# A four-layer hybrid decoder trunk: block-wise norms in the first layer, another order of the PSUM reads of x, two weight loads moved, and a new plan of the last S5 layer

## The chip, the cores and the metric

The kernel runs on one core of a Trainium2 chip. TensorE (PE) multiplies, VectorE (DVE), ScalarE (ACT) and GpSimd (POOL) do the element-wise work, and SyncE (SP) does nothing but issue DMAs, one after the other in its own order. The metric is the device time of one execution in microseconds; less is better.

## The reference

Four layers, 512 positions, width 1024, fp32. Layer 0 and layer 3 are S5, layer 1 is HGRN2, layer 2 is sliding-window attention. Each layer does:

```python
u = rms_norm(h, norm_pre[i])
y = branch(u)                      # projection, causal mixer, gate, output projection
h = h + rms_norm(y, norm_post[i])

def rms_norm(x, g):
    return x * rsqrt(mean(x * x, axis=-1) + NORM_EPS) * g

# the S5 branch
proj = h @ w_in                    # 1024 x 2048
u, z = proj[..., :1024], proj[..., 1024:]
# 64 groups of 16 channels with 64 complex states: s[t] = a * s[t-1] + B u[t]; y = Re(C s) + D u
y = gelu(y)
y = y * sigmoid(y @ w_glu + b_glu)
out = (y * silu(z)) @ w_out
```

## The kernel before, in words

**Tiles.** Positions are cut into four blocks `tb` of 128. Every layer starts with the pre-norm of its input h (in layer 0 that is x itself). `norm_stats` squares each block on ACT with a running sum (`xs`, `pre_ss`), two short POOL instructions make 1/rms from the sum (`rs_m`, `rs_r`), and DVE scales the block into `xs`. `norm_xt` transposes `xs` on PE, 128x128 at a time, into a PSUM tile `xtp` that holds four transposed pieces; there are two such tiles in turn. ACT copies each piece out of PSUM as `xh` (the leading bits, with the norm's gain), and DVE writes the rest, `xl = xtp * gain - xh`. In layer 0 there is no `xl`: ACT writes plain fp32 `xf`. Matmuls with the weights `whi`/`wlo` (split in the same way, `w_conv`: ACT writes `whi`, DVE writes `wlo`) take three passes, `xh*whi`, `xl*whi`, `xh*wlo`.

**Weights.** `w_load` issues on SP the two DMAs of one weight chunk into `wraw`, whose buffers are reused, so a load can stand in SP's queue and wait until PE has read the old contents. `w_next` hands out the next chunk, and starts the load of later ones. Layer 0's `s5_in` chunks are used as they are (`plain`); all others are split.

**S5.** The projection gives u in eight blocks b of 128 channels. For each block: SP sends u through DRAM (`ub<-ut`, `u<-ub`); DVE makes `q` (713, 715) from the parameters `prm` (a DMA) and from it and the powers `ap` the tile `vt` (727 to 731); PE multiplies `kps<-vt,c`; PE transposes (`tps`, `ktp`); DVE masks `ksb`; eight DMAs on SP spread `ksb` into the block-Toeplitz matrix `toep`; PE makes the block inputs `xps<-u,v`, DVE rotates them, runs the scan `r` (line 835) and makes `spre` (845); PE adds up `yps<-toep,u` and `yps<-w,spre` (858, 860); ACT takes it out as `ysb` (gelu), PE transposes it back (`ytp`), ACT writes `y`, `yh`. Then comes the GLU projection `pj<-yh,...`.

**Order.** Engines run their instructions strictly in the order given. In the S5 layers that order comes from a hand-made planner (`Flow`): each piece of work is a list of steps with an engine, an estimated length and the marks it needs, and has a rank; the planner always emits the step that could begin first by its estimates, the rank breaking ties. Elsewhere the order follows the tile framework's scheduler. `out_proj` of one layer is interleaved with `norm_stats` and `norm_xt` of the next, in halves (blocks 0 and 1, then 2, then 3); `first_blocks` starts the next layer's projection on the first half.

Lines that matter: 274 squares, 277 scales `xs`, 253/254 the POOL steps, 292 `xtp`, 296 `xh`/`xf`, 298 `xl`, 228 `pj`, 152 weight loads, 182/183 `whi`/`wlo`, 706 `prm`, 691/692 and 613 `rotf`, 802/806 `ub`/`u`, 773 `toep`, 718 `c` (on ACT, from `prm`), 950 `yl`.

Of the kernel before, what the change touches and what calls it, by code (L numbers as in the profile page):

```python
# [15 lines left out]
ALU = mybir.AluOpType  # L16
# [4 lines left out]
KB = 8  # L21
# [29 lines left out]
class Mark:  # L51


    def __init__(self):
        self.t = None


class Flow:
# [6 lines left out]

    LAG = {"P": 0.4, "V": 0.4, "A": 0.4, "G": 0.4, "D": 4.5}

    def __init__(self):
        self.free = dict.fromkeys(self.LAG, 0.0)
        self.lines = []  # L70

    def add(self, line, rank, t=0.0):
# [36 lines left out]
class Trunk:  # L109
# [86 lines left out]
    def w_next(self, name=None):  # L196
        i = self.wi
        if name is not None:
            assert self.wseq[i][0] == name, (self.wseq[i], name)
        self.wi += 1  # L200
        self.w_conv(i)
        self.w_load(i + 1)
        if self.wseq[i][0].endswith("out") and self.wseq[i][2] == 1:
            return self.wcv.pop(i)
        if not self.plain(i) or self.plain(i + 1):
            self.w_conv(i + 1)
            self.w_load(i + 2)
        return self.wcv.pop(i)

    def w_take(self):  # L210
# [47 lines left out]
    def norm_stats(self, L, tbs, h):  # L258

        nc = self.nc  # L260
        if tbs[0] == 0:
            if L == 0:
                self.x = (self.act.tile([P, KB, T], F32, tag="xh", name="xf"), None)
            else:
                self.x = (
                    self.act.tile([P, KB, T], F32R, tag="xh", name="xh"),
                    self.act.tile([P, KB, T], F32R, tag="xl", name="xl"),
                )
            self.xs = self.act.tile([P, 4, D], F32, tag="z", name="xs")
        xs = self.xs  # L270
        n = len(tbs)
        ss = self.small.tile([P, 2], F32, tag="pre_ss", name="pre_ss", bufs=2)
        for i, tb in enumerate(tbs):
            self.last_sq = nc.scalar.activation(out=xs[:, tb, :], in_=h[:, tb, :], func=AF.Square, accum_out=ss[:, i:i + 1])
        r = self.rstd(ss[:, 0:n], D, n)
        for i, tb in enumerate(tbs):
            self.last_xs = nc.vector.tensor_scalar(out=xs[:, tb, :], in0=h[:, tb, :], scalar1=r[:, i:i + 1], scalar2=None, op0=ALU.mult)

    def norm_xt(self, L, tbs):

# [6 lines left out]
        for k2 in range(KB // per):  # L287
# [5 lines left out]
            for kk in range(per):  # L293
                k = per * k2 + kk
                g = self.gpre[:, L * KB + k:L * KB + k + 1]
                nc.scalar.activation(out=xh[:, k, c], in_=ps[:, kk, :], func=AF.Copy, scale=g)
                if xl is not None:
                    nc.vector.scalar_tensor_tensor(out=xl[:, k, c], in0=ps[:, kk, :], scalar=g, in1=xh[:, k, c].bitcast(F32), op0=ALU.mult, op1=ALU.subtract)  # L298
            yield

# [27 lines left out]
    def out_proj(self, L, nxt, h):  # L328
# [31 lines left out]
        with self.wx_pool(L):  # L360
# [14 lines left out]
                    spill(0)  # L375
            self.w_conv(self.wi)
            self.w_load(self.wi + 1)
            xt = iter(()) if nxt is None else self.norm_xt(nxt, (0, 1))
            next(xt, None)
            for tb in (2, 3):  # L380
# [238 lines left out]

    def s5_convs(self, i0, m):  # L620

        for c in range(1, 8):
            yield "A", 2.1, (m["cd", c - 2],) if c > 1 else ()
            yield "V", 2.6, ()
            self.w_conv(i0 + c)
            self.w_load(i0 + c + 1)
            yield m["cv", c]
# [360 lines left out]
    def layer_s5(self, L):  # L988
# [6 lines left out]
        with self.scratch("left"), self.tc.manual_schedule(engines={E.PE, E.DVE, E.Activation, E.SP}):  # L995
# [2 lines left out]
            m = defaultdict(Mark)  # L998
            ps, yh, yl, glu = {}, [], [], []

            flow = Flow()
            i0 = self.wi
            if j == 0:
                flow.add(self.s5_tables(j, m), 0, 5.0)
            else:
                m["ap"].t = 4.5
                flow.add(self.s5_convs(i0, m), 60)
            for b in range(8):
                flow.add(self.s5_core(b, m), 10 * b + 1)
# [478 lines left out]
    def run(self):  # L1488
        tc, nc, a = self.tc, self.nc, self.a
        self.plan_weights()  # L1490
        with tc.tile_pool(name="cst", bufs=1) as self.small, \
# [16 lines left out]
            for tb in range(4):  # L1508
                nc.sync.dma_start(out=x0[:, tb, :], in_=a["x"][tb * 128:(tb + 1) * 128, :])
                if tb == 1:  # L1510
                    self.w_load(0)
            for tbs in ((0, 1), (2,), (3,)):
                self.norm_stats(self.layers[0], tbs, x0)
            for _ in self.norm_xt(self.layers[0], (0, 1)):
                pass
            self.hsrc = a["x"].rearrange("(b p) d -> p b d", p=P)
# [125 lines left out]
```

## Time and profile before

| | us |
|---|---|
| median of three runs | 1119.49 (1118.13 to 1121.62) |
| the profiled execution, its own time | 1116.3 |
| its span in the trace | 1114.5 |
| PE busy in the span | 1031.2 (93%) |
| DVE busy | 750.5 (67%) |
| ACT busy | 504.2 (45%) |
| mean granted TensorE clock | 0.973 of full speed |

The time before the span starts and after it ends is 1.8 us. Rows of the timeline read: start, length, engine, line, operation, output<-inputs, and, in brackets, how long the engine had been idle before and what ended that.

### The profile page before, as it was taken

The numbers are of one execution on the slowest core, as the hardware profiler recorded it, in microseconds if no ns is written. First come the engines' busy times: TensorE is split into PE (matmuls) and PEld (weight loads), VectorE is DVE, ScalarE is ACT, GpSimd is POOL, SyncE is SP. The second block draws the span as 40 slices with busy tenths as digits, with TensorE's granted clock in tenths as the row PEclk, the third lists the DMA queues.
The fourth block names the chain that finished last, engine by engine and source line by source line (L and its number), as shares of the span: only waits on it lengthen the run. The fifth ranks groups of instructions, "written<-read, shape, count | busy, mean of one in ns | idle before, by whom it ended". The sixth has DMA issues, their size and how long they took to land.

```text
span 1114.5 us, 17031 instructions
## 1 busy us (share of the span) xinstructions
PE 1031.2 (93%) x6480; PEld 822.3 (74%) x6480; DVE 750.5 (67%) x1458; ACT 504.2 (45%) x933; POOL 103.2 (9%) x162
## 2 busy tenths in 40 slices
PE   5999975999999999999999898999997879988997
PEld 4755544778899798998978885666676767766876
DVE  6786759585698777887856565556664468863752
ACT  4344425554452314333244534688743355645540
POOL 2000000030200000000011022100002010100200
PEclk9999988999999999999999999999999889998999
DMA  6574233533432324414153452211125357544331
GB/s 230 137 190 126 74 85 98 171 114 126 143 103 81 114 71 132 144 65 151 61 189 124 122 145 62 74 57 53 61 95 167 117 155 238 173 124 146 104 103 57
DMA packets 70577, 133.31 MB, mean 120 GB/s; under 512 B 28896, under 2 KB 40032, under 8 KB 69472
## 3 DMA queue, kind: packets, MB, share of 16 engines
q1 hardware_dynamic: 65664, 119.04, 34.6%
q10 hardware_dynamic: 4832, 13.19, 3.6%
q8 instruction: 51, 0.84, 0.3%
q14 instruction: 30, 0.25, 0.1%
HBM read 100.51 MB, written 20.15 MB: 108 GB/s over the span
## 4 chain that ended last, share of the span: by engine, by line
PE 63%; DVE 15%; ACT 6%; DMA 6%; issue 5%; SPq 2%; POOL 1%; ACTq 1%; DVEq 0%; POOLq 0%
PE pj L228 26%; PE ops L243 13%; PE zps L243 4%; PE vps L243 3%; PE sps L1120 2%; PE scps L1328 2%; DVE wlo L183 2%; SPq L773 2%; ACT whi L182 2%; PE aops L1364 2%; DMA rsw<-rraw 1%; DMA prm<-in_s_bc 1%; PE ptp L1359 1%; DVE sg L1049 1%; PE yps L858 1%
## 5 line engine op out<-in xcount | busy, mean ns | idle before, releaser
L183 DVE TENSOR_TENSOR wlo<-wraw,whi 128x1024 fp32r<-128x1024 f32 x116 | 143.2, 1251 | 65.0 <-ACT whi L182 56.1
L228 PE MATMUL pj<-xh,whi 128*128 128x512 f32 (+1 forms) x496 | 182.3, 370 | 0.0
L228 PE MATMUL pj<-xl,whi 128*128 128x512 f32 (+1 forms) x496 | 177.9, 360 | 2.5 <-DVE xl L298 2.4
L228 PE MATMUL pj<-xh,wlo 128*128 128x512 f32 (+1 forms) x496 | 177.4, 359 | 0.0
L182 ACT ACTIVATE whi<-wraw 128x1024 fp32r<-128x1024 f32 x116 | 120.7, 1056 | 79.4 <-PE pj L228 38.2
L228 PE MATMUL pj<-xf,wraw 128*128 128x512 f32 (+1 forms) x320 | 116.0, 512 | 0.0
L228 PEld LDWEIGHTS pj<-xh,whi 128*128 128x128 f32 x496 | 96.3, 195 | 16.8 <-issue 5.8
L228 PEld LDWEIGHTS pj<-xl,whi 128*128 128x128 f32 x496 | 96.9, 196 | 14.6 <-DVE xl L298 3.2
L228 PEld LDWEIGHTS pj<-xh,wlo 128*128 128x128 f32 x496 | 96.5, 195 | 13.6 <-issue 1.7
L243 PE MATMUL ops<-whi,gh 128*128 128x512 f32 x256 | 101.6, 398 | 2.7 <-ACT gh L1051 2.2
L243 PE MATMUL ops<-wlo,gh 128*128 128x512 f32 x256 | 100.7, 394 | 1.1 <-DVE wlo L183 1.0
L243 PE MATMUL ops<-whi,gl 128*128 128x512 f32 x256 | 100.5, 395 | 0.0
L228 PEld LDWEIGHTS pj<-xf,wraw 128*128 128x128 f32 x320 | 59.2, 192 | 40.4 <-issue 36.7
L243 PEld LDWEIGHTS ops<-whi,gh 128*128 128x128 f32 x256 | 48.2, 188 | 13.8 <-ACT gh L1051 3.0
L243 PEld LDWEIGHTS ops<-wlo,gh 128*128 128x128 f32 x256 | 48.2, 188 | 13.2 <-DVE wlo L183 2.7
L243 PEld LDWEIGHTS ops<-whi,gl 128*128 128x128 f32 x256 | 48.1, 188 | 11.3 <-DVE gl L1052 0.9
L228 PE MATMUL pj<-yl,whi 128*128 128x512 f32 x128 | 51.0, 399 | 3.5 <-DVE yl L950 3.5
L228 PE MATMUL pj<-yh,whi 128*128 128x512 f32 x128 | 51.3, 401 | 0.5 <-ACT yh L946 0.5
L228 PE MATMUL pj<-yh,wlo 128*128 128x512 f32 x128 | 50.8, 397 | 0.0
L341 DVE TENSOR_TENSOR yg<-ops,gpost 128x512 f32<-128x512 f32 x32 | 21.9, 688 | 36.9 <-ACT junk L339 36.6
L243 PE MATMUL vps<-wlo,xh 128*128 128x256 f32 x160 | 45.3, 283 | 0.0
L243 PE MATMUL vps<-whi,xl 128*128 128x256 f32 x160 | 45.3, 283 | 0.0
(279 smaller groups left out, 2106.4 us busy)
## 6 DMA issues: line engine op xcount, KB each, us to landing
wraw<-in_s_in SPq DMA_DIRECT2D x32, 512.0 KB, 6.3
wraw<-in_hg_in SPq DMA_DIRECT2D x32, 512.0 KB, 3.6
wraw<-in_at_in SPq DMA_DIRECT2D x20, 512.0 KB, 4.2
wraw<-in_s_glu SPq DMA_DIRECT2D x16, 512.0 KB, 3.8
wraw<-in_s_out SPq DMA_DIRECT2D x16, 512.0 KB, 3.5
hd<-h SPq DMA_DIRECT2D x6, 1024.0 KB, 4.0
prm<-in_s_bc SPq DMA_DIRECT2D x16, 256.0 KB, 4.6
ub<-ut SPq DMA_DIRECT2D x16, 256.0 KB, 4.2
```

Source lines behind the costliest of these rows:

```text
L182: nc.scalar.activation(out=hi, in_=raw, func=AF.Copy)
L183: nc.vector.tensor_tensor(out=lo, in0=raw, in1=hi.bitcast(F32), op=ALU.subtract)
L228: self.nc.tensor.matmul(ps, lhsT=l[k // 4][:, k % 4, c], rhs=r[:, k, n0:n1], start=k == 0 and n == 0, stop=k == KB - 1 and n == len(terms) ...
L243: self.nc.tensor.matmul(ps, lhsT=l[:, k, c], rhs=r[k // per][:, k % per, :], start=k == 0 and n == 0, stop=k == KB - 1 and n == 2)
L341: nc.vector.tensor_tensor(out=yg[:, tb, f], in0=ps, in1=gp[:, f], op=ALU.mult)
L773: nc.sync.dma_start(out=toep[128 - n:128, jj, :, :], in_=ksb[0:n].rearrange("p a g h -> p (a g) h"))
L858: nc.tensor.matmul(o, lhsT=u[:, g, :], rhs=d["toep"][:, :, g, :], start=True, stop=False)
L1049: nc.vector.tensor_tensor(out=sg, in0=sg, in1=y[:, k, :], op=ALU.mult)
L1120: nc.tensor.matmul(ps[:, c, :], lhsT=k[:, c * 128:c * 128 + 128], rhs=q4[:, c, :, 1, :], start=True, stop=True)
L1328: nc.tensor.matmul(ps[:, bb, lo:256], lhsT=self.q[r, 4 * p + 2 * b2 + bb, qs], rhs=self.k[r, p, ks], start=True, stop=True)
L1359: nc.tensor.transpose(tp[:, f, bb, :], sm[:, bb, f * 128:f * 128 + 128], self.ident)
L1364: nc.tensor.matmul(ops[64 * i:64 * i + 64].rearrange("p b q -> p (b q)"), lhsT=self.v[:, n - 1 + f, kv * 64:kv * 64 + 64], rhs=pts[i][:, f ...
```

## The change

1. `norm_xt`: for each PSUM tile, first all ACT copies (`xh`), then all DVE differences (`xl`); before, the two were written in turns, piece by piece.
2. Layer 0 only: `norm_stats` runs for one block at a time (four calls instead of blocks 0 and 1 together, then 2, then 3), and the scaling into `xs` is an ACT instruction instead of a DVE one. The second weight chunk is also loaded before the second half of x.
3. `w_next`: a plain chunk starts the split and load of later chunks only if those are plain too. In layer 0 the first GLU chunk is thus loaded one step later.
4. `out_proj` before layer 3 also splits the next weight chunk and loads the one behind it.
5. The planner of layer 3: ACT counts as busy until 12.0 and DVE until 13.0, the powers `ap` as ready at 12.0 instead of 4.5, and the weight splits of `s5_convs` start at chunk 2 instead of 1.

```diff
@@ class Flow
-    def __init__(self):
+    def __init__(self, **busy):
         self.free = dict.fromkeys(self.LAG, 0.0)
+        self.free.update(busy)
@@ def w_next
-        if not self.plain(i) or self.plain(i + 1):
+        if not self.plain(i):
             self.w_conv(i + 1)
             self.w_load(i + 2)
+        elif self.plain(i + 1):
+            self.w_conv(i + 1)
+            if self.plain(i + 2):
+                self.w_load(i + 2)
@@ def norm_stats
-            self.last_xs = nc.vector.tensor_scalar(out=xs[:, tb, :], in0=h[:, tb, :], scalar1=r[:, i:i + 1], scalar2=None, op0=ALU.mult)
+            if L == 0:
+                nc.scalar.activation(out=xs[:, tb, :], in_=h[:, tb, :], func=AF.Copy, scale=r[:, i:i + 1])
+            else:
+                self.last_xs = nc.vector.tensor_scalar(out=xs[:, tb, :], in0=h[:, tb, :], scalar1=r[:, i:i + 1], scalar2=None, op0=ALU.mult)
@@ def norm_xt
                 nc.scalar.activation(out=xh[:, k, c], in_=ps[:, kk, :], func=AF.Copy, scale=g)
-                if xl is not None:
+            if xl is not None:
+                for kk in range(per):
+                    k = per * k2 + kk
+                    g = self.gpre[:, L * KB + k:L * KB + k + 1]
                     nc.vector.scalar_tensor_tensor(out=xl[:, k, c], ...)
@@ def out_proj
             self.w_load(self.wi + 1)
+            if nxt == 3:
+                self.w_conv(self.wi + 1)
+                self.w_load(self.wi + 2)
@@ def s5_convs
-        for c in range(1, 8):
+        m["cv", 1].t = 0.0
+        for c in range(2, 8):
@@ planner of the S5 layers
-            flow = Flow()
+            flow = Flow() if j == 0 else Flow(A=12.0, V=13.0)
-                m["ap"].t = 4.5
+                m["ap"].t = 12.0
@@ start of the program
                 if tb == 1:
                     self.w_load(0)
-            for tbs in ((0, 1), (2,), (3,)):
-                self.norm_stats(self.layers[0], tbs, x0)
+                    self.w_load(1)
+            for tb in range(4):
+                self.norm_stats(self.layers[0], (tb,), x0)
```

How this moves instructions is seen at three places. In the changed kernel's rows the line numbers are its own: 279 squares, 284 scales x, 305 is `xh`/`xf`, 311 is `xl`, 735 is `c`, 815 `ut`, 832 `mdec`, 819/823 `ub`/`u`, 723 `prm`, 153 the weight loads, 790 `toep`, 183 `whi`.

ACT at the start of the program, before, from the cosine table of layer 0 to the last `xf` of the first half; `x_98` is x:

```order
L421 ACTIVATE cos<-red_n,cst 128x96
L274 ACTIVATE xs,pre_ss<-x_98 128x1024 x2
L296 ACTIVATE xf<-xtp,gpre 128x256 x4
L1031 DMA bglu<-in_s_bglu 128x8
L296 ACTIVATE xf<-xtp,gpre 128x256 x4
```

and in the changed kernel:

```order
L437 ACTIVATE cos<-red_n,cst 128x96
L284 ACTIVATE xs<-x_98,rs_r 128x1024 x2
L305 ACTIVATE xf<-xtp,gpre 128x256 x2
L279 ACTIVATE xs,pre_ss<-x_98 128x1024
L305 ACTIVATE xf<-xtp,gpre 128x256
L284 ACTIVATE xs<-x_98,rs_r 128x1024
L279 ACTIVATE xs,pre_ss<-x_98 128x1024
L305 ACTIVATE xf<-xtp,gpre 128x256
L284 ACTIVATE xs<-x_98,rs_r 128x1024
L305 ACTIVATE xf<-xtp,gpre 128x256 x4
```

Two squares and all four scalings now stand between and ahead of the eight `xf` on the one engine.

SP in layer 0, before, from the `rotf` that follows block 3's `toep` to the `prm` after block 4's:

```order
L691 DMA rotf<-rot 64x1024
L692 DMA rotf<-rot 64x1024
L152 DMA wraw<-in_s_glu 128x1024 x2
L806 DMA u<-ub 128x512
L773 DMA toep<-ksb 16x128
...
L773 DMA toep<-ksb 128x128
L706 DMA prm<-in_s_bc 128x512
```

and in the changed kernel:

```order
L708 DMA rotf<-rot 64x1024
L709 DMA rotf<-rot 64x1024
L823 DMA u<-ub 128x512
L790 DMA toep<-ksb 16x128
...
L790 DMA toep<-ksb 128x128
L723 DMA prm<-in_s_bc 128x512
L153 DMA wraw<-in_s_glu 128x1024 x2
```

The GLU load has moved behind u, the eight `toep` DMAs and `prm`.

ACT at the start of layer 3, before, from the square of the last block on (`mdec` and `c` are S5 parameters, `junk` ends out_proj's norm):

```order
L339 ACTIVATE junk,po_ss<-ops 128x512
L274 ACTIVATE xs,pre_ss<-h 128x1024
L1031 DMA bglu<-in_s_bglu 128x8
L815 ACTIVATE mdec<-m_7713 128x8x63
L718 ACTIVATE c_7724<-prm,cst 128x8x16
L296 ACTIVATE xh<-xtp,gpre 128x128 x16
L748 ACTIVATE kt<-kps 128x256
L756 ACTIVATE v<-tps 128x512
L798 ACTIVATE ut<-pj 128x512
```

and in the changed kernel:

```order
L352 ACTIVATE junk,po_ss<-ops 128x512
L279 ACTIVATE xs,pre_ss<-h 128x1024
L1049 DMA bglu<-in_s_bglu 128x8
L305 ACTIVATE xh<-xtp,gpre 128x128 x16
L832 ACTIVATE mdec<-m_7730 128x8x63
L815 ACTIVATE ut<-pj 128x512
L735 ACTIVATE c_7741<-prm,cst 128x8x16
L183 ACTIVATE whi<-wraw 128x1024 x2
L815 ACTIVATE ut<-pj 128x512
```

The sixteen `xh` of blocks 2 and 3 now stand ahead of `mdec` and `c`. On DVE the same has happened, before:

```order
L277 TENSOR_SCALAR xs<-h,rs_r 128x1024
L713 TENSOR_TENSOR q_7805<-prm,co 128x256
L715 TENSOR_TENSOR q_7805<-q_7805,q12b 128x256
L727 TENSOR_TENSOR vt<-ap,q_7805 128x1024
L298 SCALAR_TENSOR_TENSOR xl<-xtp,gpre,xh 128x128 x8
L730 TENSOR_TENSOR t_7874<-ap,q_7805 128x1024
L731 TENSOR_TENSOR vt<-vt,t_7874 128x1024
L298 SCALAR_TENSOR_TENSOR xl<-xtp,gpre,xh 128x128 x8
```

and in the changed kernel:

```order
L286 TENSOR_SCALAR xs<-h,rs_r 128x1024
L311 SCALAR_TENSOR_TENSOR xl<-xtp,gpre,xh 128x128 x16
L730 TENSOR_TENSOR q_7931<-prm,co 128x256
L732 TENSOR_TENSOR q_7931<-q_7931,q12b 128x256
L744 TENSOR_TENSOR vt<-ap,q_7931 128x1024
L747 TENSOR_TENSOR t_7978<-ap,q_7931 128x1024
L748 TENSOR_TENSOR vt<-vt,t_7978 128x1024
```

The first `q`, `vt` and `t` of layer 3 come behind all sixteen `xl`.

## Rows read from the trace of the kernel before

**Rows 1.** The windows of the trace, busy time of each engine in five stretches (PE, PEld, DVE, ACT, POOL, each with its count of instructions), then the granted clock, the DMA share and GB/s: first the start, then layer 0 up to its block 4, then the end of layer 2's projection, the head of layer 3, and the rest of layer 3's mixer.

```profile
0.00:12.00 12.00, 0.06 (x1) 0.07 (x1) 4.28 (x18) 7.01 (x13) 4.41 (x22) 1.00 0.84 310
...
30.00:141.00 111.00, 110.26 (x688) 64.04 (x688) 82.49 (x106) 43.61 (x78) 5.80 (x10) 1.00 0.50 132
...
840.00:860.00 20.00, 16.19 (x119) 14.85 (x117) 10.05 (x14) 5.25 (x12) 5.78 (x16) 1.00 0.57 158
860.00:874.00 14.00, 8.83 (x47) 7.35 (x48) 9.04 (x20) 5.08 (x15) 0.62 (x1) 0.52 0.34 125
874.00:1016.00 142.00, 124.62 (x1101) 100.48 (x1100) 91.96 (x116) 80.67 (x127) 12.76 (x15) 0.97 0.60 179
```

**Rows 2.** The waits of PE, from 0 to 300 us: who waited for whom, us in total, times, longest.

```profile
PE xtp L292 <- DVE xs L277: 11.9, 1, 11.9
PE yps L858 <- DMA toep<-ksb: 9.1, 2, 7.6
```

**Rows 3.** The waits of PE, from 840 to 1045 us.

```profile
PE xtp L292 <- DVE xl L298: 6.4, 2, 4.9
PE kps L745 <- DVE vt L731: 5.3, 1, 5.3
PE pj L228 <- DVE yl L950: 3.5, 1, 3.5
```

**Rows 4.** The timeline of ACT at the start of the program (the square of block 2, then the first `xf`), of POOL (the mask, then the 1/rms of block 2), of DVE (block 2's scaling), and of PE (first transposes, the first half's matmuls, the next transposes).

```profile
11.03 1.06 ACT L274 ACTIVATE xs<-x 128x1024 f32<-128x1024 f32 x1 [1.23 <-DMA x<-in_x]
...
13.54 0.84 ACT L296 ACTIVATE xf<-xtp,gpre 128x256 f32<-128x256 f32 x2
...
9.50 0.40 POOL L766 TENSOR_TENSOR dmx<-dm,cst 128x128 f32<-128x128 f32 x1 [5.94 <-DMA cst<-in_const]
...
12.26 0.33 POOL L253 TENSOR_SCALAR rs_m<-pre_ss 128x1 f32<-128x1 f32 x1 [1.23 <-ACT xs L274]
...
13.25 0.75 DVE L277 TENSOR_SCALAR xs<-x,rs_r 128x1024 f32<-128x1024 f32 x1 [0.71 <-POOL rs_r L254]
...
11.94 2.21 PE L292 MATMUL xtp<-cst,xs 128*128 128x128 f32 x8 [11.94 <-DVE xs L277]
...
16.79 10.38 PE L228 MATMUL pj<-xf,wraw 128*128 128x256 f32 x46
27.00 1.04 PE L292 MATMUL xtp<-cst,xs 128*128 128x128 f32 x8
```

**Rows 5.** Layer 0, block 4: the timeline of SP, of DVE (the masked `ksb`; the last part of the scan's output `spre`), and of PE (a group of `yps` of block 3; the first of block 4).

```profile
122.83 19.52 SPq L152 DMA_DIRECT2D wraw<-in_s_glu  x2
...
142.91 5.00 SPq L773 DMA_DIRECT2D toep<-ksb  x8
...
131.84 0.29 DVE L768 TENSOR_TENSOR ksb<-ktp,dmx 128x128 f32<-128x128 f32 x1 [6.01 <-PE ktp L762]
...
141.37 0.68 DVE L845 TENSOR_TENSOR spre<-r,rsw 128x504 f32<-128x504 f32 x1
...
122.62 0.39 PE L858 MATMUL yps<-toep,u 128*64 128x128 f32 x4
...
149.59 0.69 PE L858 MATMUL yps<-toep,u 128*64 128x128 f32 x4 [7.62 <-DMA toep<-ksb]
```

**Rows 6.** The windows behind that, columns as in rows 1.

```profile
144.00:150.00 6.00, 0.41 (x4) 0.44 (x6) 5.16 (x8) 0.00 (x0) 0.00 (x0) 0.76 0.58 173
150.00:156.00 6.00, 6.00 (x41) 4.63 (x38) 0.00 (x0) 1.19 (x2) 0.00 (x0) 0.68 0.42 118
```

**Rows 7.** The timeline of PE where layers 1 and 2 begin (transposes of block 3), and the windows behind these.

```profile
306.54 0.66 PE L292 MATMUL xtp<-cst,xs 128*128 128x128 f32 x4 [2.59 <-DVE xl L298]
...
623.41 0.77 PE L292 MATMUL xtp<-cst,xs 128*128 128x128 f32 x5 [3.37 <-DVE xl L298]
...
306.00:312.00 6.00, 5.46 (x32) 5.18 (x33) 5.30 (x25) 4.94 (x13) 0.00 (x0) 0.72 0.00 1
...
624.00:630.00 6.00, 5.98 (x38) 5.74 (x37) 2.80 (x8) 2.88 (x8) 0.00 (x0) 0.72 0.00 1
```

**Rows 8.** The head of layer 3: the timeline of ACT (`c`, then the `xh` of block 2), of DVE (`xl`), of PE.

```profile
856.43 0.40 ACT L718 ACTIVATE c<-prm,cst 128x128 f32<-128x128 f32 x1 [4.58 <-DMA prm<-in_s_bc]
856.74 0.35 ACT L296 ACTIVATE xh<-xtp,gpre 128x128 fp32r<-128x128 f32 x1
859.45 0.37 ACT L296 ACTIVATE xh<-xtp,gpre 128x128 fp32r<-128x128 f32 x1 [2.36 <-DVE xl L298]
...
861.02 0.62 ACT L296 ACTIVATE xh<-xtp,gpre 128x128 fp32r<-128x128 f32 x2 [0.42 <-DVE xl L298]
...
859.85 0.35 DVE L298 SCALAR_TENSOR_TENSOR xl<-xtp,gpre,xh 128x128 fp32r<-128x128 f32 x1 [0.43 <-ACT xh L296]
...
861.83 1.11 PE L292 MATMUL xtp<-cst,xs 128*128 128x128 f32 x4 [4.87 <-DVE xl L298]
...
867.54 0.58 PE L228 MATMUL pj<-xl,whi 128*128 128x256 f32 x1 [1.76 <-DVE xl L298]
```

**Rows 9.** The timeline of DVE and of PE in layer 3, blocks 1 and 2, and of PE where the GLU's matmuls begin.

```profile
894.61 0.42 DVE L713 TENSOR_TENSOR q<-prm,co 128x256 f32<-128x256 f32 x1 [10.79 <-DMA prm<-in_s_bc]
...
905.49 1.08 PE L745 MATMUL kps<-vt,c 128*32 128x128 f32 x16 [5.32 <-DVE vt L731]
...
1015.48 0.80 PE L228 MATMUL pj<-yl,whi 128*128 128x512 f32 x1 [3.45 <-DVE yl L950]
```

## The prediction

> **What bounds the kernel now.** I first read the windows, for where PE stands still [rows 1]. From 30 to 141 us PE is busy 110.26 of 111 us, so whatever delays the start delays everything up to there. Layer 3 is the opposite: PE is idle 20.00 - 16.19 = 3.8 us at the end of the norm before it, 14.00 - 8.83 = 5.2 us in its head and 142.00 - 124.62 = 17.4 us in the rest of its mixer, 26.4 us together, and the head runs at a granted clock of 0.52, close to the lower of the two levels (1.2 of 2.4 GHz). Then I read PE's waits. Up to 300 us there are the first 11.9 us for x and, among others, 7.6 us in one wait for `toep` [rows 2]. In layer 3 they are transposes behind `xl`, `kps` behind `vt`, the GLU behind `yl` [rows 3]. The timelines then tell what stood in front of each awaited thing. Elsewhere the change touches PE only through the order of PSUM reads where layers 1 and 2 begin [rows 7].
>
> **The start of layer 0: a loss.** The first transposes began at 11.94, the 23 matmuls of blocks 0 to 2 ran without a gap from 16.79, and the next transposes stood at 27.00: (27.00 - 16.79) / 23 = 0.444 us each [rows 4]. In the changed order ACT does, after the cosine: two scalings, two `xf`, a square, an `xf`, a scaling, a square, an `xf`, a scaling, four `xf`. Splitting the sums of blocks 0 and 1 gives nothing, since POOL's 1/rms stands behind its mask, which waited for the constants until 9.50. A scaling on ACT I take at the 1.06 us of the square with the same shape; an `xf` is 0.84 / 2 = 0.42. From the end of a square to the scaling that uses it take 13.25 - (11.03 + 1.06) = 1.16 us, which is ACT's accumulator, POOL's two steps and the hand-over [rows 4]. With that: scalings to 12.7 (11.0 at the earliest, two of 1.06, overlapping a little), transposes, `xf` 0 and 1 from 13.5 to 14.4; square of block 2 to 15.5; `xf` 2 to 15.9; scaling of block 2 from 16.65 to 17.7; square of block 3 to 18.8; `xf` 3 to 19.2; scaling from 20.0 to 21.0; `xf` 4 from there, done at 21.45. PE's last four first-half transposes need the PSUM tile that `xf` 3 empties, so PE idles from about 16 to 19.2, does three matmuls of block 0 and waits again for `xf` 4. From 21.45 there are still 4 + 16 = 20 matmuls: 21.45 + 20 x 0.444 = 30.3 against 27.0, **+3.3 us**. The second weight chunk ahead of x's second half costs its 1 MB at 310 GB/s [rows 1], 3.4 us on block 2 of x (before, ACT took it at 11.03 on arrival): 14.4, just where ACT now wants it, so nothing more. DVE is freed of four scalings, but PE waits for none of DVE's work here: no gain.
> Such a pause lowers the clock: behind a PE gap of 2.59 us at 306.54 the next six microseconds showed a granted clock of 0.72, behind 3.37 us at 623.41 again 0.72 [rows 7], which is 6 x 0.28 = 1.7 us lost each time. Here two gaps of 3 and 1 us follow on a short activity. I add 1.3, between 0 (the one gap at 11.94 cost little) and 1.7 twice. Start: **+4.6**, from +2.5 (scalings as short as DVE's 0.75) to +6.7. The Trainium skill (TensorE: Matmul & The Clock Gate, Part 1: The HAM clock gate) speaks against this part: the throttled clock is the default and activity has to release it. By it a PE that stops in its first ten microseconds pays a low clock again; the rows at 306.54 and 623.41 agree, and the term would be nearer +5.
>
> **The GLU load moved behind `toep` in layer 0: a gain.** Block 4's `ksb` was ready at 131.84 + 0.29 = 132.1, but SP issued its `toep` only at 142.91, because the GLU load in front took 19.52 us from 122.83: its second half waited for a `wraw` buffer that PE was still reading. PE then stood still for 7.62 us until 149.59 [rows 5]. Behind it the clock was 0.76 and 0.68 in two six-microsecond windows, the first with PE idle [rows 6]; a group of `yps` took 0.69 instead of 0.39 [rows 5]. On 6.00 busy us at 0.68 that is 6.00 x 0.32 = 1.9 us. In the changed order u, the eight `toep` and `prm` precede the load. `toep` can go out at 132.2, its issue takes 5.00 [rows 5], and it lands by about 139, ahead of PE's arrival at 141.97. PE's next need, `spre`, is ready at 141.37 + 0.68 = 142.05: no new wait. The load itself then blocks the next block's u, which before went out after it as well. Gain **-9.3** (rounded down from 7.6 + 1.9), lower end 0 if something else on SP or DVE is late next, upper end -9.5. The Trainium skill (DMA: Bandwidth & Descriptors, Anatomy of one DMA) says that DMA engines don't wait on semaphores, the issuing sequencer does, before dispatch. The 19.52 us row agrees: one waiting load holds up all behind it.
>
> **PSUM reads, layers 1 and 2.** In turns, an `xh` comes every 860.2 - 859.45 = 0.78 us (ACT's idle 0.42 <-`xl` between two of 0.37), DVE idles 0.43 for each `xh`; two ACT copies without that wait take 0.62 for both, 0.31 each [rows 8]. Four pieces of a PSUM tile in turns are some 3.1 us; all `xh`, then all `xl`, some 1.2 + 0.2 + 1.2 = 2.6, and ACT goes on to the other tile meanwhile, so two tiles take about 1.2 + 2 x 1.2 + 0.4 = 4.0 instead of 6.2. Against it the first `xl` comes later by three copies, 0.9 us. Where layer 1 begins the wait was 2.59, in layer 2 3.37 with a table function between the copies [rows 7]. I take **-0.5** (0 to -1.5) and **-2** (0 to -3.5).
> The Trainium skill (PSUM — Partial Sum Buffer, PSUM bank collisions raise a hardware error) says that two engines must not touch one bank of the same partitions at once, reads included, so each alternation is a hand-over. The 0.42 and 0.43 us between the two engines agree. By it one tile's `xl` can't overlap its own `xh`, only the other tile's.
>
> **Layer 3.** The pool is 26.4 us of idle PE, plus 8.83 x 0.48 = 4.2 us of slow clock in the head, plus at most 142 x 0.03 = 4.3 in the rest [rows 1]: 34.9. In the head, ACT's first `xh` of block 2 waited behind `c`, which waited for `prm` until 856.43, and DVE put `vt` between: one `xh` at 856.74, the next at 859.45, then the slow alternation, transposes at 861.83, the first matmul with the new `xl` at 867.54 [rows 8]. Now all sixteen `xh` come ahead of `c`, all sixteen `xl` ahead of `q` and `vt`. The transposes of block 2 end about 853, its tiles are emptied by 856.5, block 3 follows, and the matmuls run from 859: 8.5 us earlier and without most of the slow clock, -12. Behind that, blocks come forward: `prm` of the later block, which held DVE until 894.61 and PE until 905.49 [rows 9], now stands ahead of more weight loads. Following the new order with row durations, I still find these waits on PE: 1.5 in the head, 2 for the first block's `spre`, 3 for the second's `toep`, 4 for `vt` of blocks 5 and 6, 6.5 at the last block (only nine `pj` and one `yps` group stand between its `xps` and its `yps`, while rotation, scan and `spre` run), 1 for `ytp`, and 2.5 of clock behind the longest: 20.5. That gives 20.5 - 34.9 = -14.4. Counting from the other side, step by step to the GLU's first matmul, I got 994.5 against 1015.5 [rows 9], -21. I take **-17**, with -8 and -25 as ends. Chunk 2's earlier split adds no instruction; it is hidden in the head.
>
> **Sum.** 4.6 - 9.3 - 0.5 - 2 - 17 = -24.2 on the profiled 1116.3, 1092.1. The median of the runs is 1119.5, 3.2 above that execution, so **1095**.
>
> **Rivals.**
> - *The blocks set the pace of layer 3.* For: DVE works 91.96 us of the 142, and waits for `toep` and `prm` on one SP queue; the head's gain then turns into waits later. Against: most of DVE's idle is itself a wait for the head. Only the head's 12 less 4 returned: -8, sum -15, 1104. Chance 0.16.
> - *The `toep` wait of layer 0 stays under another name*, the change not doing what it seems to: another DMA or `spre` is late at the same point. Against: the rows give three microseconds of room. Sum -24.2 + 9.3 = -15, 1104. Chance 0.09.
> - *The start costs far more:* a PE that is never long busy until 21 us stays at the low level of the clock, and 20 matmuls of 0.444 at half speed add at most 8.9 to the 3.3. In the rows a low clock behind a pause cost 1.7 [rows 7], so the chance is 0.06; the sum is -24.2 - 4.6 + 12.2 = -17, 1103. The clock-gate section of the Trainium skill named above would have it so.
> - *Slower:* SP in layer 3. Chunk loads now stand ahead of `prm`, u and `toep` of several blocks; if a load waits for its buffer as the GLU load did (19.52 us, price 7.6 + 1.9 = 9.5), each such place costs 9.5. Without that the sum is -24; three such places cancel it, a fourth decides: 4 x 9.5 - 24 = +14, 1133. For: the row of 19.52 shows the mechanism. Against: in the old order two loads stood ahead of `prm` too, and the price there was the one 5.3 of `kps` [rows 3, 9]. Chance 0.03.
>
> **How the numbers follow.** Forecast 0.66, rivals 0.16, 0.09, 0.06 and 0.03. The forecast's own ends: start +2.5 with layer 3 at -25 gives about 1083; the other ends and the first three rivals reach to 1104 and a little above. Range 1083 to 1107, which leaves out the slower rival and combinations of two. A measurement of this kernel tells 0.3%, about 3.4 us, from nothing. All but the last case lie beyond that on the fast side; I leave 0.95 faster, 0.02 for losses that just cancel, 0.03 slower.
>
> **What would show it.** In the new trace: PE idle near 16 to 21 us and the transposes after the first blocks at about 30; no wait of PE for `toep` near 142 to 150; the first layer-3 matmul with the second half's `xl` near 859 on the old scale (some 854 after the shifts); the GLU's first matmul some 17 us earlier relative to that layer's start, with a wait of 5 or more us just before the last `yps`. Wrong would be a `toep` wait in layer 0 above 3 us, or a layer-3 mixer as long as before.

## The result and the profile after

The changed kernel took 1088.82 us (median of four runs, 1087.09 to 1091.9), the kernel before 1119.28 us in its four. The ratio is 0.9728, 95% interval 0.9701 to 0.9756: 27 to 33 us less. The profiled execution of the changed kernel took 1089.59 us with a span of 1087.8; in spans the gain is 1114.5 - 1087.8 = 26.7 us.

Where it came from is read best by following the same landmarks of PE through both timelines (start in us, before and after):

| PE's first ... | before | after | shift | won or lost since the row above |
|---|---|---|---|---|
| `kps` of layer 0 | 42.52 | 47.22 | +4.70 | +4.70, the start |
| `ops` of layer 0 (out_proj) | 243.20 | 239.36 | -3.84 | -8.54, layer 0's blocks |
| `vps` of layer 1 | 320.69 | 314.02 | -6.67 | -2.83, the transition to layer 1 |
| transposes for layer 2 | 594.73 | 587.23 | -7.50 | -0.83 |
| `vps` of layer 2 | 637.62 | 626.94 | -10.68 | -3.18, the transition to layer 2 |
| transposes for layer 3 | 829.95 | 820.03 | -9.92 | +0.76 |
| `pj<-xl` of the second half, layer 3 | 867.54 | 848.10 | -19.44 | -9.52, the head |
| `pj<-yl` of the GLU, layer 3 | 1015.48 | 989.83 | -25.65 | -6.21, the mixer's blocks |
| `ops` of layer 3 | 1061.45 | 1034.76 | -26.69 | -1.04 |

Each column is one execution. How far two executions of the same kernel can differ over one stretch is seen in e10: 3.2 us.

**The start.** ACT's timeline of the changed kernel, from the square of block 2 on (start, length, line, operation):

```profile
13.71 1.05 ACT L279 ACTIVATE xs<-x 128x1024 f32<-128x1024 f32 x1
...
14.74 0.47 ACT L305 ACTIVATE xf<-xtp,gpre 128x256 f32<-128x256 f32 x1
15.87 1.15 ACT L284 ACTIVATE xs<-x,rs_r 128x1024 f32<-128x1024 f32 x1 [0.65 <-POOL rs_r L259]
16.93 1.04 ACT L279 ACTIVATE xs<-x 128x1024 f32<-128x1024 f32 x1
...
17.96 0.45 ACT L305 ACTIVATE xf<-xtp,gpre 128x256 f32<-128x256 f32 x1
19.27 1.15 ACT L284 ACTIVATE xs<-x,rs_r 128x1024 f32<-128x1024 f32 x1 [0.86 <-POOL rs_r L259]
...
20.33 1.55 ACT L305 ACTIVATE xf<-xtp,gpre 128x256 f32<-128x256 f32 x4
```

and PE's beside it:

```profile
15.37 1.91 PE L233 MATMUL pj<-xf,wraw 128*128 128x256 f32 x4
18.47 1.11 PE L301 MATMUL xtp<-cst,xs 128*128 128x128 f32 x4 [1.19 <-ACT xf L305]
...
20.84 11.03 PE L233 MATMUL pj<-xf,wraw 128*128 128x256 f32 x40 [0.40 <-ACT xf L305]
31.70 1.04 PE L301 MATMUL xtp<-cst,xs 128*128 128x128 f32 x8
```

The last four `xf` end at 20.33 + 1.55 = 21.9, behind two squares and two scalings, and 0.65 and 0.86 us of waiting for POOL. The next transposes, at 27.00 in [rows 4], stand at 31.70: 4.7 us later. Of the last 40 records, which are 20 matmuls, none waits, yet they take 31.70 - 20.84 = 10.86 us and not 20 x 0.444 = 8.88: 2.0 us of slow clock, read from the durations (the last section says why not from the column of the clock).

**The GLU load behind `toep`.** SP's timeline, PE's first `yps` of block 4, and a window (busy time of PE, PEld, DVE, ACT, POOL, then the granted clock, the DMA share, GB/s):

```profile
136.86 5.00 SPq L790 DMA_DIRECT2D toep<-ksb  x8
141.97 0.52 SPq L723 DMA_DIRECT2D prm<-in_s_bc  x1
142.53 4.51 SPq L153 DMA_DIRECT2D wraw<-in_s_glu  x2
...
146.61 0.44 PE L875 MATMUL yps<-toep,u 128*64 128x128 f32 x4
...
141.00:160.00 19.00, 19.00 (x124) 10.01 (x123) 16.32 (x23) 6.81 (x12) 1.16 (x2) 1.00 0.46 125
```

`toep` goes out at 136.86, and PE reaches the `yps` at 146.61 without a wait. Against [rows 5] no 7.62 us are left, and against [rows 6] the clock is 1.00. A group takes 0.44 instead of 0.69. The load now takes 4.51 us to issue, and nobody waits for what stands behind it.

**The transitions to layers 1 and 2.** PE's waits in the timeline, and the windows behind them, columns as above:

```profile
302.88 0.39 PE L233 MATMUL pj<-xl,whi 128*128 128x256 f32 x1 [1.05 <-DVE xl L311]
...
613.39 0.66 PE L301 MATMUL xtp<-cst,xs 128*128 128x128 f32 x4 [0.84 <-DVE xl L311]
614.65 0.50 PE L233 MATMUL pj<-xh,whi 128*128 128x256 f32 x2 [0.60 <-ACT xh L305]
...
303.00:309.00 6.00, 6.00 (x51) 6.00 (x52) 3.86 (x17) 3.42 (x5) 0.00 (x0) 1.00 0.02 5
614.00:620.00 6.00, 5.39 (x44) 5.16 (x44) 2.62 (x10) 2.98 (x9) 0.00 (x0) 1.00 0.11 22
```

Where [rows 7] have 2.59 and 3.37 us and a clock of 0.72 behind each, there are 1.05 us (a matmul behind the first `xl`) and 0.84 with another 0.60 behind an `xh`, and the clock stays at 1.00.

**Layer 3.** The three windows that answer to [rows 1]:

```profile
830.00:850.00 20.00, 18.94 (x144) 17.77 (x142) 11.14 (x25) 8.59 (x25) 5.54 (x16) 1.00 0.54 153
850.00:864.00 14.00, 14.00 (x118) 13.10 (x117) 7.32 (x9) 5.78 (x9) 0.80 (x1) 1.00 0.66 208
864.00:990.00 126.00, 112.67 (x999) 88.57 (x998) 93.74 (x117) 72.05 (x117) 10.39 (x13) 0.95 0.60 174
```

PE's idle time in the head is gone (14.00 of 14.00, before 8.83), at a clock of 1.00 instead of 0.52. The stretch to the GLU takes 126 instead of 142 us and still holds 126.00 - 112.67 = 13.3 us of idle PE. ACT, DVE and PE in the head:

```profile
842.78 2.18 ACT L305 ACTIVATE xh<-xtp,gpre 128x128 fp32r<-128x128 f32 x8 [2.53 <-PE xtp L301]
...
843.96 2.16 DVE L311 SCALAR_TENSOR_TENSOR xl<-xtp,gpre,xh 128x128 fp32r<-128x128 f32 x8 [1.88 <-ACT xh L305]
...
848.10 0.39 PE L233 MATMUL pj<-xl,whi 128*128 128x256 f32 x1 [0.78 <-DVE xl L311]
```

ACT does eight copies in 2.18 us, DVE its eight in 2.16, where [rows 8] show one every 0.78. What is left in layer 3 is in PE's waits, by line, 805 to 1030 us (total, times, longest), to be put beside [rows 3]:

```profile
PE yps L877 <- DVE spre L862: 5.2, 2, 4.9
PE kps L762 <- DVE vt L748: 3.7, 1, 3.7
PE yps L875 <- DMA toep<-ksb: 3.5, 2, 2.7
PE pj L233 <- DVE xl L311: 1.0, 2, 0.8
```

The longest is at the last block. PE, then ACT, and the windows there:

```profile
980.68 0.44 PE L875 MATMUL yps<-toep,u 128*64 128x128 f32 x4 [0.84 <-DMA toep<-ksb]
986.06 0.69 PE L877 MATMUL yps<-w,spre 128*64 128x128 f32 x4 [4.94 <-DVE spre L862]
...
980.17 1.99 ACT L183 ACTIVATE whi<-wraw 128x1024 fp32r<-128x1024 f32 x2
...
982.69 0.63 ACT L856 ACTIVATE rsw<-r 64x512 f32<-64x512 f32 x1
...
982.00:986.00 4.00, 0.00 (x0) 0.00 (x0) 3.58 (x6) 3.95 (x8) 0.00 (x0) 0.79 0.62 194
986.00:990.00 4.00, 3.94 (x30) 3.52 (x31) 3.61 (x7) 1.28 (x4) 0.00 (x0) 0.50 0.20 79
```

PE has its `toep` and stands until 986.06 for `spre`. ACT splits a weight chunk from 980.17 while the scan's `rsw`, which `spre` needs, comes behind it at 982.69. The clock falls to 0.50 behind the pause.

### The profile page after: what moved, and what is told of

Its sections match the earlier page's. It is cut to its first block, busy times and chain, and to the rows that moved or that the text cites. A ratio compares the mean times of both kernels' runs of the same rounds, so it can differ in the third digit from the quotient of the medians.

```text
span 1087.8 us, 17048 instructions
## 1 busy us (share of the span) xinstructions
PE 1027.0 (94%) x6480; PEld 816.6 (75%) x6480; DVE 746.8 (69%) x1454; ACT 505.2 (46%) x937; POOL 104.4 (10%) x164
## 4 chain that ended last, share of the span: by engine, by line
PE 66%; DVE 14%; ACT 7%; DMA 5%; issue 5%; POOL 2%; SPq 2%; ACTq 1%; DVEq 0%; POOLq 0%
PE pj L233 27%; PE ops L248 14%; PE zps L248 4%; PE vps L248 3%; PE sps L1138 3%; DVE wlo L184 3%; PE scps L1346 3%; ACT whi L183 2%; PE aops L1382 2%; DMA rsw<-rraw 1%; PE yps L877 1%; SPq L790 1%; PE yps L875 1%; PE ptp L1377 1%; DVE sg L1067 1%
## 5 line engine op out<-in xcount | busy, mean ns | idle before, releaser
L233 PE MATMUL pj<-xh,whi 128*128 128x512 f32 (+1 forms) x496 | 179.9, 364 | 1.2 <-ACT xh L305 0.6
L233 PE MATMUL pj<-xl,whi 128*128 128x512 f32 (+1 forms) x496 | 175.1, 354 | 2.1 <-DVE xl L311 2.1
L233 PE MATMUL pj<-xf,wraw 128*128 128x512 f32 (+1 forms) x320 | 119.6, 524 | 0.4 <-ACT xf L305 0.4
L233 PEld LDWEIGHTS pj<-xh,whi 128*128 128x128 f32 x496 | 93.8, 190 | 17.5 <-issue 5.4
L233 PEld LDWEIGHTS pj<-xl,whi 128*128 128x128 f32 x496 | 94.4, 190 | 13.9 <-DVE xl L311 2.9
L233 PEld LDWEIGHTS pj<-xh,wlo 128*128 128x128 f32 x496 | 94.2, 190 | 13.5 <-issue 1.7
```

The source lines that it names most:

```text
L233: self.nc.tensor.matmul(ps, lhsT=l[k // 4][:, k % 4, c], rhs=r[:, k, n0:n1], start=k == 0 and n == 0, stop=k == KB - 1 and n == len(terms) ...
```

## Experiments

Each of the first four is one part of the change put into the kernel before. Times are compared with runs of the kernel before on the same chip. e1 to e4, e5 to e8, and e9 with e10 ran on three different chips, so across these groups, and with the changed kernel, the ratios are compared and not the times.

**e1, the order of the PSUM reads alone.**

```diff
@@ norm_xt of the kernel before
-                if xl is not None:
+            if xl is not None:
+                for kk in range(per):
+                    ...
```

> The kernel before with the new order of PSUM reads alone (all xh of a tile, then all xl). Theory: where layers 1 and 2 begin, the pause of PE and the low clock behind it go together, some -3 us each, as the changed kernel's trace shows there; in layer 3 the copies still stand behind c, which waits for prm, so the head gains at most 3 us. Total -6 to -9 us, ratio 0.992 to 0.995. Rival, the two terms as predicted: -2.5 us, ratio 0.998, and the rest of the shift in layers 1 and 2 belongs to another part of the change.

Measured: 1109.41 us, ratio 0.9906 (0.9882 to 0.9930), some 10.5 us (8 to 13; the theory had 6 to 9). PE's wait where layer 1 begins and the window behind it, then the same in layer 2:

```profile
306.28 0.38 PE L228 MATMUL pj<-xl,whi 128*128 128x256 f32 x1 [0.64 <-DVE xl L302]
...
306.00:312.00 6.00, 5.72 (x47) 5.72 (x48) 3.86 (x19) 3.83 (x9) 0.00 (x0) 1.00 0.03 7
...
618.15 0.51 PE L228 MATMUL pj<-xh,whi 128*128 128x256 f32 x2 [0.88 <-ACT xh L296]
...
618.00:624.00 6.00, 5.85 (x36) 5.85 (x37) 2.25 (x8) 2.36 (x9) 0.00 (x0) 0.72 0.08 23
```

The pause of 2.59 is down to 0.64 and the clock is 1.00 where it was 0.72; the landmark behind the transition moved by -3.28, as in the changed kernel (-2.83). In layer 2 the clock was still 0.72 in one window, and only 1.7 us came from there. The pauses there were 0.83 and 0.88 us, in the changed kernel 0.84 and 0.60: a difference of 0.3 us of idle PE, and behind it 1.5 us of time. The same split shows in the other runs with this order of reads: e5 and e9, with 0.8 and 0.88, keep the low clock and gain 1.6 us there, e6 to e8, with 0.8 to 1.0 and 0.60, lose it and gain 3.0 to 3.2. That the 0.3 us decide is seen in all seven executions, but not tested by itself. In layer 3 the head of e1 is 4.8 us shorter, where at most 3 were expected. The rival, the terms as predicted, is out: its ratio of 0.998 lies outside the interval, and where the clock didn't fall, the pause and the slow clock behind it went together. The time gained by the runs (10.5) is more than the traces compare (spans 1114.5 and 1107.9); e10 comes back to that.

**e2, layer 0's start alone.**

```diff
@@ start of the program, kernel before (with norm_stats' scaling on ACT in layer 0)
                     self.w_load(0)
+                    self.w_load(1)
-            for tbs in ((0, 1), (2,), (3,)):
-                self.norm_stats(self.layers[0], tbs, x0)
+            for tb in range(4):
+                self.norm_stats(self.layers[0], (tb,), x0)
```

> The kernel before with layer 0's new start alone (squares by block, scaling on ACT, second weight chunk ahead of x's second half). Theory: PE has no slack up to block 4, and the GLU load that blocks SP waits for PE itself, so the start's loss goes through to the end: first kps 4.7 us later, total +4 to +5 us, ratio 1.004. Rival: the wait for toep in block 4 (7.6 us) absorbs it, total 0 to +1.

Measured: 1124.54 us, ratio 1.0042 (1.0012 to 1.0071), slower by 1 to 8 us; the first `kps` at 47.41, 4.9 later. The wait for `toep` doesn't absorb it:

```profile
154.51 0.69 PE L862 MATMUL yps<-toep,u 128*64 128x128 f32 x4 [7.62 <-DMA toep<-ksb]
```

It is as long as before, 7.62 us, only later, since the load that blocks SP waits for PE itself: it stands in SP's timeline for 19.51 us from 127.74, before for 19.52 from 122.83. The theory holds.

**e3, the moved GLU load alone.**

```diff
@@ w_next of the kernel before
-        if not self.plain(i) or self.plain(i + 1):
+        if not self.plain(i):
             self.w_conv(i + 1)
             self.w_load(i + 2)
+        elif self.plain(i + 1):
+            self.w_conv(i + 1)
+            if self.plain(i + 2):
+                self.w_load(i + 2)
```

> The kernel before with the moved GLU load of layer 0 alone. Theory: the 7.6 us wait for toep and the low clock behind it go, nothing takes their place: -9 to -10 us, ratio 0.991 to 0.992. Rival: another DMA or spre is late next at the same place: a wait of 3 us or more remains there and the total is above -6.

Measured: 1111.57 us, ratio 0.9926 (0.9901 to 0.9951), 5 to 11 us; the theory's 9 to 10 lie inside, the runs don't tell them from 6. At the first `ops` of layer 0 PE was 9.83 us ahead of the kernel before, and its waits of layer 0 hold no `toep` above 1.3, so the rival's wait of 3 us isn't there. At that place the theory's number is right. Of the lead, 6.8 us were gone at the end of this one profiled execution, most of them in layer 3; see e10.

**e4, layer 3's plan alone.**

```diff
@@ the kernel before
+            if nxt == 3:
+                self.w_conv(self.wi + 1)
+                self.w_load(self.wi + 2)
-            flow = Flow()
+            flow = Flow() if j == 0 else Flow(A=12.0, V=13.0)
-                m["ap"].t = 4.5
+                m["ap"].t = 12.0
-        for c in range(1, 8):
+        m["cv", 1].t = 0.0
+        for c in range(2, 8):
```

> The kernel before with the parts for layer 3 alone (planner with busy ACT and DVE, early chunk 2), PSUM reads in turns as before. Theory: most of layer 3's gain comes from the order (xh and xl ahead of c, q, vt), and the turns cost some 3 to 6 us of it: -11 to -14 us, ratio 0.987 to 0.990. Rival: the PSUM order carries the head, since sixteen pieces in turns take 12.6 us at 0.785 each: -5 us or less, ratio 0.995 or more.

Measured: 1104.85 us, ratio 0.9872 (0.9853 to 0.9891), some 14 us. ACT in the head, one `xh` out of the sixteen:

```profile
853.75 0.37 ACT L297 ACTIVATE xh<-xtp,gpre 128x128 fp32r<-128x128 f32 x1 [0.42 <-DVE xl L299]
```

The sixteen copies no longer wait for `prm`, but they still alternate with DVE, one every 0.78 us, from 852.97 to 863.5. From the transposes for layer 3 to the GLU's first `yl` the trace won 9.2 us here, and 15.7 in the changed kernel. So the plan carries the larger part of layer 3. That the order of reads brings the rest is by subtraction: over the same stretch it alone wins 1.0 us in e1's trace and 1.8, with the early chunk, in e9's, so by the traces most of the missing 6.5 us comes only where both are there (e1's execution lost 4.4 us of its own at a place that e10 looks at).

**e5 to e7, what costs in the new start.** All three contain the rest of the change.

```diff
@@ e5: the changed kernel with the start and the DVE scaling of the kernel before
@@ e6: the changed kernel
-            for tb in range(4):
+            for tb in range(2):
                 self.norm_stats(self.layers[0], (tb,), x0)
             for _ in self.norm_xt(self.layers[0], (0, 1)):
                 pass
+            for tb in (2, 3):
+                self.norm_stats(self.layers[0], (tb,), x0)
@@ e7: the changed kernel
-            if L == 0:
-                nc.scalar.activation(out=xs[:, tb, :], in_=h[:, tb, :], func=AF.Copy, scale=r[:, i:i + 1])
-            else:
-                self.last_xs = nc.vector.tensor_scalar(...)
+            self.last_xs = nc.vector.tensor_scalar(...)
```

> The changed kernel with layer 0's old start (no ACT scaling, sums of blocks 0 and 1 together, second weight chunk behind x). Theory: the start's loss of 4.7 us is separate and goes through to the end: first kps at 42.5 instead of 47.2, total 4 to 5 us under the changed kernel, ratio to before 0.968 to 0.970. Rival: with the toep wait gone the loss is taken up in the waits of layer 0's later blocks (kps behind vt, 9.1 us), ratio 0.972 to 0.973 as with the change.

> The whole change, but in layer 0 the transposes and xf of blocks 0 and 1 are written ahead of the norms of blocks 2 and 3, so that ACT does one square instead of two squares and two scalings between and ahead of the eight xf. Theory: what stood ahead of the xf on ACT is the whole loss of the start: first kps at 41 to 43 instead of 47.2, ratio 0.966 to 0.970. Rival: the loss comes from scaling on ACT or from x's second half behind 1 MB of weights: first kps stays at 46 to 47, ratio 0.972 to 0.973.

> The whole change, but x is scaled by DVE as before (sums by block and the early second weight chunk stay). Theory: the scalings and the 1.2 us wait for POOL ahead of each, which stood between the xf on ACT, carry the loss; two squares alone cost little: first kps at 42.5 to 44. Rival: the late arrival of x's second half or the sums by block carry it: first kps at 46 to 47.

Measured: e5 1085.83 us, ratio 0.9686 (0.9672 to 0.9701); e6 1083.70 us, ratio 0.9671 (0.9648 to 0.9694); e7, one run, 1083.66 us. The transposes that stood at 31.70 in the changed kernel, in e5, e6 and e7:

```profile
26.21 1.04 PE L297 MATMUL xtp<-cst,xs 128*128 128x128 f32 x8
```

```profile
26.32 1.04 PE L301 MATMUL xtp<-cst,xs 128*128 128x128 f32 x8
```

```profile
26.05 1.04 PE L297 MATMUL xtp<-cst,xs 128*128 128x128 f32 x8
```

All three are at 26 us and their first `kps` at 41.6 to 41.8, 5.5 us ahead of the changed kernel. By the runs, e5's ratio is 0.0042 under the changed kernel's, 4.7 us, as its theory said; its own profiled execution, at the upper end of its runs, had 2.4 us of the lead left at the end. e6 keeps the scaling on ACT, the sums by block and the early second weight chunk, so none of these costs anything by itself. Its theory holds: what stood ahead of the `xf` on ACT was the whole loss. e7 tells which part: it keeps the two squares ahead of the last four `xf` and takes only the scalings away, and the loss is gone. So the squares alone cost nothing here (`kps` at 41.56, where 42.5 to 44 were expected), and it takes the two scalings of blocks 2 and 3 with their waits for POOL. Whether these would cost as much without the squares no run shows. None of the parts of the new start brings a gain that the runs can tell: e5 and e6 overlap.

**e8, e6 with another order at the last block of layer 3.**

```diff
@@ s5_core, behind the second rsw
+        yield m["rw", b]
@@ s5_glu_first
-            yield "V", 2.6, (m["rest"],)
+            yield "V", 2.6, (m["rest"], m["rw", 7]) if early else (m["rest"],)
```

> As e6, and in layer 3 the split of the second GLU chunk may not start before the last block's rsw: on ACT the two whi (2.0 us) then stand behind rsw. Theory: the wait of the last yps for spre, 4.9 us in the changed kernel, shrinks to 2 to 2.5 us, and less low clock follows: 3 to 4 us under e6, ratio 0.963 to 0.966. Rival: the wait only turns into one for the GLU's second chunk (pj behind wlo), as long as what was won: within 1 us of e6.

Measured: 1082.93 us, ratio 0.9655 (0.9637 to 0.9673), not to be told from e6. PE at the last block:

```profile
979.49 0.69 PE L878 MATMUL yps<-w,spre 128*64 128x128 f32 x4 [3.27 <-DVE spre L863]
...
983.44 0.66 PE L893 MATMUL ytp<-cst,ysb 128*128 128x128 f32 x4 [0.70 <-ACT ysb L884]
```

The wait for `spre` shrank from 4.94 (5.08 in e6) to 3.27, less than expected, and a transpose now waits 0.70 us. From the transposes for layer 3 to the GLU the trace is 1.6 us shorter than e6's. The rival, a wait for the second GLU chunk, didn't show either; the gain is too small to measure. e6 and e8 beat both kernels: the upper ends of their ratios, 0.9694 and 0.9673, lie under the lower end of the changed kernel's, 0.9701.

**e9, the planner's old times.**

```diff
@@ e5, layer 3
-            flow = Flow() if j == 0 else Flow(A=12.0, V=13.0)
+            flow = Flow()
-                m["ap"].t = 12.0
+                m["ap"].t = 4.5
```

> As e5 (the change without the new start), but the planner of layer 3 keeps its old times (ap at 4.5, ACT and DVE free at 0); the early chunk 2 stays. On ACT mdec and c then stand ahead of the sixteen xh again. Theory: the planner's times carry layer 3's gain: the first matmul with block 2's xl comes some 6 to 9 us later relative to the layer's start, and 9 to 13 us of e5's gain go, ratio 0.977 to 0.981. Rival: the early chunk carries it, since weight loads stood between rotf and prm: ratio 0.968 to 0.972, as e5.

Measured: 1098.94 us, ratio 0.9799 (0.9760 to 0.9839), 13 us of e5's gain gone. ACT and PE in the head:

```profile
841.82 0.40 ACT L730 ACTIVATE c<-prm,cst 128x128 f32<-128x128 f32 x1 [4.66 <-DMA prm<-in_s_bc]
842.12 2.16 ACT L300 ACTIVATE xh<-xtp,gpre 128x128 fp32r<-128x128 f32 x8
...
849.33 0.58 PE L232 MATMUL pj<-xl,whi 128*128 128x256 f32 x1 [1.32 <-DVE xl L306]
```

ACT waits 4.66 us for `prm`, and the `xh` stand behind that. Yet the first `pj<-xl` comes at 849.33, 32.9 us after layer 3's first transposes, in the changed kernel 28.1: the head loses 4.8 us, less than expected, and the blocks behind it lose the rest (with `kps<-vt` 4.3 and `pj<-yl` 3.4 among the waits). The early chunk 2, here with the new order of reads, brings next to nothing without the planner's times: from the transposes to the GLU the trace is 1.8 us shorter than before. The theory holds, the split between head and blocks was put wrongly.

**e10, the kernel before once more.**

> The kernel before, profiled once more. Theory: its first profiled execution was a short one, since in e1, e2 and e3, whose layer 3 has almost the same order, the last yps group of block 5 waits 2.7 us for spre (behind a prm that landed late) and the GLU begins 4.4 us later, which the first profile doesn't show: here the wait is there too and the time 1119 to 1122 us. Rival: the parts of the change brought that wait about: no such wait here, 1115 to 1118 us.

Measured: 1115.3 us in the profiled execution, 1119.85 us as the median of the timed runs of the same kernel beside it. The theory as written fell: the wait is 0.77 us here, and the time under 1119. Both are what the rival said, so that the parts of the change brought the wait about in e1 to e3 isn't ruled out. What the executions differ in, SP, DVE and PE in e3 and then here:

```profile
954.56 0.38 SPq L710 DMA_DIRECT2D prm<-in_s_bc  x1
...
964.11 0.42 DVE L717 TENSOR_TENSOR q<-prm,co 128x256 f32<-128x256 f32 x1 [4.20 <-DMA prm<-in_s_bc]
...
969.90 0.70 PE L864 MATMUL yps<-w,spre 128*64 128x128 f32 x4 [2.80 <-DVE spre L849]
```

```profile
960.46 0.38 SPq L706 DMA_DIRECT2D prm<-in_s_bc  x1
...
968.14 0.43 DVE L713 TENSOR_TENSOR q<-prm,co 128x256 f32<-128x256 f32 x1 [2.31 <-DMA prm<-in_s_bc]
...
973.93 0.69 PE L860 MATMUL yps<-w,spre 128*64 128x128 f32 x4 [0.77 <-DVE spre L845]
```

`prm` of the same block lands 9.55 us after its issue in e3 and 7.68 here (DVE's wait for it ends then). DVE, which must do `q` first, comes to `spre` later, and PE waits 2.80 instead of 0.77 us. The two profiles of before have 6.85 and 7.68, with waits of 0.22 and 0.77. From the `xps` of that block to the next `kps` PE takes 4.4 us more in e3 than in the first profile of before, the same in e1 (`prm` 9.48, wait 2.74) and 5.1 in e2 (10.03, 2.73).

But the wait isn't all of that. This execution takes 3.2 us more over the same stretch, with a wait only 0.55 longer, because its clock was low there. The window in the first profile, then here:

```profile
976.00:982.00 6.00, 4.59 (x58) 3.64 (x57) 5.90 (x8) 2.16 (x3) 0.00 (x0) 1.00 0.99 313
```

```profile
974.00:980.00 6.00, 6.00 (x40) 5.20 (x40) 5.90 (x7) 0.60 (x1) 0.00 (x0) 0.58 0.87 252
```

And its time is no longer for it. So executions with almost the same order differ by 3 to 5 us at this one place, by the late `prm` and by the low clock behind PE's pauses, but that doesn't explain why both profiled executions of the kernel before lie 3.2 and 4.6 us under the median of its timed runs. That stays open, and so does what makes `prm` slow.

## Why the prediction was right, and where it was off

The forecast was 1095 in a range from 1083 to 1107; it came out 6 us lower, inside the range.

- **The start:** +4.6 forecast, +4.70 in the trace, +4.7 by e2's runs (1.3 to 8). The steps came out as written down: `xf` 3 done at 18.4 (19.2 forecast), the four last `xf` from 20.33 (21.0), PE's 20 matmuls from 20.84 (21.45). The earlier steps were a little faster, the slow clock a little dearer: 2.0 us where 1.3 had been put, so two small errors cancel. The Trainium skill (TensorE: Matmul & The Clock Gate, Part 1: The HAM clock gate) says that the throttled clock is the default and activity releases it. These durations agree: 0.43 us a record up to about 25 us, then 0.222.
- **The GLU load:** -9.3 forecast; e3's trace has -9.83 at the end of layer 0, the changed kernel -8.54. The difference of about 0.8 between forecast and changed kernel lies behind the 9.1 us wait of `kps`: PE is 5.0 us ahead of before at its end and 3.9 at the next `toep` wait, and the clock was low for longer in between: 0.52 and 0.80 in the two windows of ten microseconds from 175 us, before 0.56 and 0.93 in those from 180.
- **The transitions:** -0.5 and -2 forecast, -2.83 and -3.18 measured, with e1 confirming the first (-3.28). This is the term of the sum that was mis-sized. The text had worked out 1.7 us of slow clock behind each pause, and used it against the start only; where the pause gets short enough it goes as well. In layer 2 that was close: in e1, e5 and e9 nearly the same order left 0.3 us more of a pause, and the slow clock stayed.
- **Layer 3:** -17 forecast, -16.8 measured (from -9.92 to -26.69). That it is so close is in part luck: the -17 was chosen between two counts of its own, -14.4 and -21, and its parts miss in opposite directions. Its two halves: the head gave 9.5 where 12 was put, the blocks 7.3 where 5 was left. The waits that were said to stay are there almost by name: 4.94 + 0.84 at the last block (6.5 forecast), 2.7 for `toep` (3), 3.7 for `vt` (4), 0.8 in the head (1.5). The 2 us for the first block's `spre` and the 1 for `ytp` are not (0.3 and none). Idle PE in the three windows is 14.4 us where the listed waits make 18, while the slow clock takes up to 126 x 0.05 = 6.3 where 2.5 were put; together 20.7, against 20.5.
- **From the profile to the median:** this step failed most. 3.2 us were added because the profiled execution of before lay that far under its median, as if the changed kernel's would too. But the changed kernel's lies 0.8 above its median (1089.59 and 1088.82), and why the profiled executions of before are short stays open (e10). Without that addition the sum would have said 1092, and with the transitions at 6 instead of 2.5, 1088.6. In spans the forecast was -24.2, the trace has -26.7.
- **The rivals:** the blocks didn't give back the head's gain, they added to it. The `toep` wait did not stay under another name. The start's clock cost 2.0, not 8.9. The loads in front of `prm` in layer 3 made no stall on PE of the size that was feared (9.5): its longest wait there is 4.94, for `spre`.
- **Two slips in the working:** a start of +2.5 with layer 3 at -25 adds up to 1085, not 1083, which takes the transitions' ends as well; and 860.2 - 859.45 is 0.75, the 0.78 comes from the next `xh` in the trace at 860.23. Neither moves the forecast.

The parts add up: -10.5, +4.7, -8.3 and -14.3 by the runs of e1 to e4 are -28.4, against -30.5 for the whole; each of the five is known to 2 or 3 us only, so this says that nothing large is missing, not more.

## What to carry to other kernels

Price a pause of TensorE with the slow matmuls behind it, and price it the same way where a change takes a pause away as where it makes one. Two engines that read the same tile in turns pay a hand-over for every piece: let one of them go through the whole tile first. On an issuing queue that runs strictly in order, a load whose buffer is not yet free is as good as a wait for all behind it, so put it behind whatever is needed sooner. And don't add the offset between one profiled execution and the median to a forecast: the changed kernel's profile need not lie off its median by the same.

## What had not been expected of the hardware

At the very start of the program the column of the granted clock doesn't show the slow clock: the windows from 12 to 36 us of the changed kernel all say 1.00. The trace's entries of the granted clock begin only at 25.2 us there (17.4 in the kernel before), at full speed, and the column counts the time ahead of the first entry as full. The durations do show it: a matmul record, 0.222 us at full speed, starts every 0.43 us from 21.42 to 24.84, and four transposes take 1.11 us at 18.47, where eight take 1.04 at 31.70. The kernel before has the same at 11.94 [rows 4], 2.21 us for eight.

Two pauses of less than a microsecond each can cost more than their length. Where layer 2 begins, pauses of 0.83 and 0.88 us were followed by a window at 0.72 (e1), pauses of 0.84 and 0.60 by one at 1.00 (the changed kernel).

A parameter load of 256 KB took between 6.85 and 10.03 us from issue to landing at the same place of nearly the same order. The later it landed, the longer PE took from the `xps` of that block to the next `kps`, slow clock included: 8.2 us at 6.85, 11.3 at 7.68, 12.6 at 9.48 and 9.55, 13.3 at 10.03.
